# A hybrid decoder trunk on one core: S5 steps let in by VectorE's account, and initial states copied by ScalarE

## The chip, the cores and the metric

The kernel runs on one core of one Trainium2 chip. The metric is the device time of one execution in microseconds (us), as the median of the runs shown; lower is better. The profile is of one execution of its own. Engines: PE is TensorE (with its weight loads as PEld), DVE is VectorE, ACT is ScalarE, POOL is GpSimd, and SP is the engine that issues most DMAs.

## The reference, cut to what matters

Two layers (DEPTH 2) run over 256 prompt tokens and 8 sample streams of 4 tokens, 288 tokens in all, with a model width of 2048, in float32.

```python
def _layer(x, ...):
    z = x @ w_in
    u, cv, cg = z[..., :1024], z[..., 1024:2048], z[..., 2048:]
    y5, h_re, h_im = _s5(u, h0_re, h0_im, ...)   # diagonal complex state space, 64 groups x 64 states
    g5 = gelu(y5); s5_out = g5 * sigmoid(g5 @ s5_w_glu)
    c = silu(_ln(_causal_dwconv(cv * sigmoid(cg), conv_buf, conv_w, conv_b)))   # width 31
    x = _ln(ALPHA * x + concatenate([s5_out, c]) @ w_out)
    gate, val = split(_causal_dwconv(x @ ffn_w_up, ffn_buf, ...))               # width 3
    x = _ln(ALPHA * x + (silu(gate) * val) @ ffn_w_down)
    x = _ln(ALPHA * x + sigmoid(x @ pe_w_gate) * (p @ pe_w))
```

The S5 part is h[t] = a h[t-1] + B u[t], y = Re(C h) + D u, with complex a. The prompt starts at h = 0; each sample stream starts at its own state h0.

## The kernel before

**Weights.** All weights stream through SBUF in units of eight 128x128 blocks (512 KB), `wraw`, with four buffers. ScalarE rounds a unit to `whi` (L202) and VectorE makes the rest `wlo` (L145, the line of a helper that records every VectorE instruction). A block costs three matmuls on 288 columns (L379, L384, L385). The first ten units of layer 0 go without a split, in plain float32 matmuls (L375).

**Order.** One Python program writes the order of every engine's queue by hand. It keeps three accounts in nanoseconds. `pe_t` is TensorE's: 400 for a block, 485 for a plain one, 1000 for `inject`, 1500 for `project`, 400 for `s5_steps`, 500 for each of the 8 steps of a convolution. `dve_t` adds up VectorE's instructions and is what S5 steps pay with. `dve_c` says when VectorE would be done with all that it was given:

```python
cost = 150.0 + (2.1 if name == "tensor_tensor_scan" else 1.05) * n
self.core.dve_c = max(self.core.dve_c, self.core.pe_t) + cost
```

So `dve_c - pe_t` is the length of VectorE's list by the account. Until now it only decides when the load of the next `wraw` is written into SP's queue (`freed`).

**S5.** Beside the weight blocks runs a generator, `s5`. Every second block, `tick` (L259 and after) first runs timers (`at`), then lets the generator make steps while its budget `scan[2]` is above zero; the budget grows with `pe_t` at `rate` (3 during the set-up in layer 0, then 1.05 and 0.9 in the two layers). A step that has nothing to do yields None and ends the loop until the next tick. The S5 width is cut in 8 chunks `c`. A chunk goes through: the tables `em`, `om`, `kp` from raw weights (layer 0 only; in layer 1 they were made ahead during the FFN of layer 0 and are loaded); `load_u`; `inject` (PE, `bu`); `scan` (DVE: two products with a rotation `stb`, a scan, two products, then the shifted states `hin`); `project` (PE, `y`); `gelu`; a trip through DRAM (`y_d`) back into `u32`. `scan` waits until `project` of the chunk before is in the queue, `inject` of the next chunk follows `scan`, and `project(c)` waits until the table of the chunk has come back (`state["o"]`): two timers of 7000 and 8000 after the copies `om` (L973), which themselves wait for `project(c-1)`.

The initial states of the 8 sample streams are put into the last 8 columns of `hin`: two GpSimd copies of 128x32 per chunk (L1029), then VectorE writes the other columns.

**Around it.** The same stretch holds the Conformer part: per chunk two products, a GLU on VectorE into `cbuf` (L145), its trip through DRAM (POOL: `cb_d`, `stack`), and a convolution on TensorE (L1215, L1218). After the last S5 chunk come the half-GLU matmuls (`g`), which need each chunk's gelu output split into `xh`, `xl`; `finish(scan)` and `xs_g` run the generator without asking for its budget if it is late. Layer 0's S5 stretch lies at about 58 to 240 us, layer 1's at about 1423 to 1584 us.

Of the kernel before, what the change touches and what calls it, by code (L numbers as in the profile page):

```python
# [10 lines left out]
AF = mybir.ActivationFunctionType  # L11
# [39 lines left out]
RATE = (1.05, 0.9)  # L51
SETUP_RATE = 3
BANK = 1400.0
TICK = 2
U_LAG = 8000.0
BACK_LAG = 7000.0
# [102 lines left out]
class Core:  # L159
# [60 lines left out]
    def next_block(self):  # L220
        s, o = divmod(self.pos, SB)
        if o == 0:
# [4 lines left out]
            self.sub.pop(s - 1, None)  # L227
        if o % TICK == 0:
            if s < NATIVE:
# [29 lines left out]
    def tick(self):  # L259
        for x in self.late:  # L260
            x[0] -= 1
        while self.late and self.late[0][0] <= 0:
            self.late.pop(0)[1]()
        while self.freed and self.freed[0][1] <= self.pe_t:
            self.stream_dma(self.freed.pop(0)[0])
        self.run_timed()
        if self.scan:
            self.scan[2] = min(self.scan[2] + self.rate * (self.pe_t - self.pe_l), BANK)
            while self.scan and self.scan[2] > 0 and self.step(self.scan):
                pass  # L270
        self.pe_l = self.pe_t
        for b in list(self.bg):
            if b is self.scan:
                continue
            b[2] = min(b[2] + b[1], 2 * b[1])
            while b[2] > 0 and self.step(b):
                pass
# [582 lines left out]
    def s5(self, l, mp):  # L860

        nc, a = self.nc, self.a
        V, G = self.V, nc.gpsimd
        N4 = 4 * NCH

        def once(n, shp):
            return mp.tile(shp, F32, name=n, tag=n, bufs=1)
        fin = once("fin", [P, NPAIR, 2, 9])
        h0 = once("h0", [P, NPAIR, 2, NB])
# [6 lines left out]
        H = once("hin", [P, 2, 4, NCH])  # L876
# [9 lines left out]
        def work(shp):  # L886
            while finals:
                finals.pop(0)()
            n = 1
            for d in shp[1:]:  # L890
                n *= d
            t = mp.tile([P, 2 * N4], F32, tag="sw", name="sw", bufs=4)[:, :n]
            if len(shp) == 3:
                return t.rearrange("p (a b) -> p a b", b=shp[2])
            return t.rearrange("p (a b c) -> p a b c", b=shp[2], c=shp[3])
# [111 lines left out]
        def scan(c, v, tb):  # L1007
            shp = [P, 2, N4]
            cosb, sinb = [tb[:, k:k + 1].to_broadcast(shp) for k in range(2)]
            A, B = work(shp), work(shp)  # L1010
            V.tensor_tensor(A, v[:, :, :N4], cosb, OP.mult)
            V.tensor_tensor(B, v[:, :, :N4], sinb, OP.mult)
            yield 1.0
            V.tensor_tensor(A[:, 0], A[:, 0], B[:, 1], OP.add)
            V.tensor_tensor(A[:, 1], A[:, 1], B[:, 0], OP.subtract)
            yield 1.0
            Af = A.rearrange("p r t -> p (r t)")
            V.tensor_tensor_scan(Af, d0.rearrange("p r q n -> p (r q n)"), Af, 0.0, OP.mult, OP.add)
            yield 1.0
            V.tensor_tensor(B, A, cosb, OP.mult)  # L1020
            yield 1.0
            V.tensor_tensor(A, A, sinb, OP.mult)
            yield 1.0
            Av, Bv = [t.rearrange("p r (q n) -> p r q n", n=NCH) for t in (A, B)]
            e = SEQ // STEP
            while state["p"] < c - 1:
                yield None
            for i in range(2):
                G.tensor_copy(H[:, i, :, e:], h0[:, 4 * c:4 * c + 4, i])  # L1029
            V.tensor_tensor(H[:, 0, :, 1:e], Bv[:, 0, :, 0:e - 1], Av[:, 1, :, 0:e - 1], OP.subtract)  # L1030
            V.tensor_tensor(H[:, 1, :, 1:e], Av[:, 0, :, 0:e - 1], Bv[:, 1, :, 0:e - 1], OP.add)
            yield 1.0

            def final():
                f = fin[:, 4 * c:4 * c + 4]
                G.tensor_tensor(f[:, :, 0, 0:1], Bv[:, 0, :, e - 1:e], Av[:, 1, :, e - 1:e], OP.subtract)
                G.tensor_tensor(f[:, :, 1, 0:1], Av[:, 0, :, e - 1:e], Bv[:, 1, :, e - 1:e], OP.add)
                for i in range(2):
                    G.tensor_tensor(f[:, :, i, 1:], f[:, :, i, 1:], Bv[:, i, :, e:], OP.add)
            finals.append(final)  # L1040
# [63 lines left out]
        def main():  # L1104
            if l == 0:
                yield from self.wait(M0_LAG)
            G.memset(om, 0.0)
            tb = tables(0)
            initial()
            for c in range(S5C):  # L1110
                while c not in ready or state["e"] < c:
                    yield None
                self.rate = RATE[l]
                v = inject(us[c])
                state["i"] = c
                yield from self.wait(PS_LAG)
                yield from scan(c, v, tb)
                if c + 1 < S5C:
                    tb = tables(c + 1)
                streams.insert(0, tail(c, us.pop(c)))  # L1120
# [511 lines left out]
```

## Time and profile before

| what | value |
|---|---|
| median of 3 runs | 2739.69 us (2739.51 to 2741.52) |
| profiled execution, its own time | 2743.43 us |
| span in its profile | 2741.6 us |
| mean granted TensorE clock | 0.991 |
| busy share: PE, DVE, ACT, POOL | 97%, 66%, 49%, 11% |

The span runs from the first to the last instruction. A granted clock of 1.00 is 2.4 GHz, and 0.50 is 1.2 GHz; a window's value between them is a mean. Idle time of an engine is put down to the instruction or DMA that ended the wait ("<-"); "issue" means that nothing which the profile shows ended it.

### The profile page before, as it was taken

The numbers are of one execution on the slowest core, as the hardware profiler recorded it, in microseconds if no ns is written. First come the engines' busy times: TensorE is split into PE (matmuls) and PEld (weight loads), VectorE is DVE, ScalarE is ACT, GpSimd is POOL, SyncE is SP. The second block draws the span as 40 slices with busy tenths as digits, with TensorE's granted clock in tenths as the row PEclk, the third lists the DMA queues.
The fourth block names the chain that finished last, engine by engine and source line by source line (L and its number), as shares of the span: only waits on it lengthen the run. The fifth ranks groups of instructions, "written<-read, shape, count | busy, mean of one in ns | idle before, by whom it ended". The sixth has DMA issues, their size and how long they took to land. (4 is left out here: it accounts for less than half of the span.)

```text
span 2741.6 us, 57943 instructions
## 1 busy us (share of the span) xinstructions
PE 2660.2 (97%) x23696; PEld 2600.8 (95%) x23696; DVE 1808.4 (66%) x3016; ACT 1352.9 (49%) x2224; POOL 305.0 (11%) x913
## 2 busy tenths in 40 slices
PE   8898999999999999999998899999999999999997
PEld 7887999999999999999987889999999999999997
DVE  6885768665677546667876558676546664566686
ACT  3453547553455345546464435565435553455363
POOL 3442001000011000000034410010000000000000
PEclk9999999999999999999999999999999999999998
DMA  7988444456566654554468775445554555455442
GB/s 236 254 249 248 151 153 162 162 192 190 186 190 197 201 167 159 174 172 153 164 191 257 229 204 180 154 159 171 175 169 157 169 174 171 156 169 176 164 151 102
DMA packets 188042, 496.12 MB, mean 181 GB/s; under 512 B 46369, under 2 KB 72241, under 8 KB 187521
## 3 DMA queue, kind: packets, MB, share of 16 engines
q1 hardware_dynamic: 174592, 444.00, 49.9%
q0 software_dynamic: 13184, 48.42, 6.2%
q8 instruction: 186, 3.05, 0.5%
q14 instruction: 80, 0.65, 0.1%
HBM read 472.11 MB, written 24.87 MB: 181 GB/s over the span
## 5 line engine op out<-in xcount | busy, mean ns | idle before, releaser
L379 PE MATMUL acc<-xh,whi 128*128 128x288 f32 x4656 | 1377.4, 296 | 8.1 <-ACT e L1333 3.2
L384 PE MATMUL acc<-xl,whi 128*128 128x288 f32 x4357 | 1288.0, 296 | 4.6 <-issue 3.7
L385 PE MATMUL acc<-xh,wlo 128*128 128x288 f32 x4357 | 1286.4, 295 | 0.0
L202 ACT ACTIVATE whi<-wraw 128x1024 fp32r<-128x1024 f32 x766 | 791.8, 1051 | 344.7 <-PE acc L384 206.1
L145 DVE TENSOR_TENSOR wlo<-wraw,whi 128x1024 fp32r<-128x1024 f32 x766 | 921.3, 1225 | 41.6 <-ACT whi L202 23.9
L379 PEld LDWEIGHTS acc<-xh,whi 128*128 128x128 f32 x4656 | 877.7, 189 | 15.8 <-ACT e L1333 4.1
L385 PEld LDWEIGHTS acc<-xh,wlo 128*128 128x128 f32 x4357 | 820.5, 188 | 3.9 <-issue 3.9
L384 PEld LDWEIGHTS acc<-xl,whi 128*128 128x128 f32 x4357 | 820.7, 188 | 3.0 <-DVE xl L145 2.5
L379 PE MATMUL acc<-hh,whi 128*128 128x288 f32 x1408 | 416.3, 296 | 0.0
L145 DVE SCALAR_TENSOR_TENSOR fo<-fe,parf,fo 128x304 f32<-128x304 f32 x352 | 188.2, 535 | 323.0 <-ACT fo L1366 316.6
L385 PE MATMUL acc<-hh,wlo 128*128 128x288 f32 x1312 | 387.7, 296 | 0.0
L384 PE MATMUL acc<-hl,whi 128*128 128x288 f32 x1312 | 386.9, 295 | 0.0
L379 PEld LDWEIGHTS acc<-hh,whi 128*128 128x128 f32 x1408 | 265.2, 188 | 0.5
L384 PEld LDWEIGHTS acc<-hl,whi 128*128 128x128 f32 x1312 | 247.0, 188 | 0.0
L385 PEld LDWEIGHTS acc<-hh,wlo 128*128 128x128 f32 x1312 | 246.6, 188 | 0.0
L1362 ACT ACTIVATE fe<-acc 128x256 f32<-128x256 f32 x176 | 67.4, 383 | 290.2 <-PE acc L385 290.2
L1372 POOL COPY fstage<-fe 128x9 f32<-128x9 f32 x176 | 44.5, 253 | 1038.1 <-ACT fe L1363 1016.7
L438 ACT ACTIVATE ln_q<-x 128x288 f32<-128x288 f32 x90 | 40.1, 446 | 221.1 <-DVE x L145 221.1
L1366 ACT ACTIVATE fo<-fe,parf 128x304 f32<-128x304 f32 x176 | 113.1, 642 | 16.7 <-ACT fe L1363 0.4
L145 DVE TENSOR_TENSOR x<-x,acc 128x288 f32<-128x288 f32 x64 | 29.1, 454 | 139.1 <-PE acc L385 139.0
L1386 ACT ACTIVATE hh<-fth 128x288 fp32r<-128x288 f32 x88 | 39.2, 445 | 163.5 <-DVE fth L145 163.5
L145 DVE SCALAR_TENSOR_TENSOR x<-x,acc 128x288 f32<-128x288 f32 x64 | 29.0, 453 | 122.9 <-PE acc L385 122.8
(251 smaller groups left out, 2340.7 us busy)
## 6 DMA issues: line engine op xcount, KB each, us to landing
wraw<-in_wts_dram SPq DMA_DIRECT2D x776, 512.0 KB
stack<-cb_d POOLq DMA_DIRECT2D x32, 282.0 KB, 9.3
cw<-in_convw_dram POOLq DMA_DIRECT2D x16, 512.0 KB, 5.3
big<-cb_d POOLq DMA_DIRECT2D x24, 282.0 KB, 9.6
cbuf<-in_convi_dram POOLq DMA_DIRECT2D x16, 283.5 KB, 9.6
cb_d<-cbuf POOLq DMA_DIRECT2D x16, 283.5 KB, 3.6
out_dram<-cb_d POOLq DMA_DIRECT2D x16, 283.5 KB, 11.5
sbt<-in_s5b_dram SPq DMA_DIRECT2D x15, 256.0 KB
```

The source lines that it names most:

```text
L145: return f(out, *args, **kw)
L202: self.nc.scalar.activation(hi, self.raw[s], AF.Copy)
L379: nc.tensor.matmul(out, w[0], xh, start=first, stop=False)
L384: nc.tensor.matmul(out, w[0], xl, start=False, stop=False)
L385: nc.tensor.matmul(out, w[1], xh, start=False, stop=last)
L438: nc.scalar.activation(st["q"], v, AF.Square)
L1362: nc.scalar.activation(e[:, 2:2 + SEQ], acc[:, :SEQ], AF.Copy)
L1366: nc.scalar.activation(o[:, :w], e[:, 2:EW], AF.Identity, bias=self.prm("ffn_conv_b", m), scale=self.prm("ffn_conv_w2", m))
L1372: nc.gpsimd.tensor_copy(stage[:, z, :, 0], e[:, SEQ:EW:6])
L1386: nc.scalar.activation(hh[i], h, AF.Copy, scale=0.5)
```

## The change

The loop in `tick` gets one more condition: a step of S5 is made only while VectorE's list by the account is under 7000 ns. The two copies of initial states go from GpSimd to ScalarE. Nothing else changes; the steps of `finish` and `xs_g` and of the generator that makes layer 1's tables ahead don't ask for the new condition.

```diff
+BACKLOG = 7000.0
 ...
-            while self.scan and self.scan[2] > 0 and self.step(self.scan):
+            while self.scan and self.scan[2] > 0 and self.dve_c - self.pe_t < BACKLOG and self.step(self.scan):
                 pass
 ...
             for i in range(2):
-                G.tensor_copy(H[:, i, :, e:], h0[:, 4 * c:4 * c + 4, i])
+                nc.scalar.activation(H[:, i, :, e:], h0[:, 4 * c:4 * c + 4, i], AF.Copy)
```

## Rows read from the trace of the kernel before

**Rows 1.** What TensorE waited for, 58 to 240 us: total, times, longest.

```profile
PE bu L399 <- ACT em L947: 4.9, 4, 4.0
PE bu L399 <- DMA ust<-u_d: 4.2, 3, 2.9
...
PE bu L399 <- DMA tm<-k_d: 2.0, 1, 2.0
PE y L399 <- ACT kp L812: 1.6, 1, 1.6
```

**Rows 2.** Windows: length, busy us of PE, PEld, DVE, ACT, POOL, clock, DMA share, GB/s.

```profile
58.00:83.00 25.00, 22.35 (x361) 21.23 (x361) 21.17 (x38) 8.57 (x14) 10.35 (x19) 0.93 1.00 276
83.00:108.00 25.00, 20.87 (x289) 19.65 (x288) 21.80 (x37) 11.27 (x21) 9.87 (x22) 0.86 0.94 259
...
128.00:153.00 25.00, 20.55 (x389) 17.34 (x388) 17.66 (x35) 10.81 (x21) 10.04 (x19) 0.93 0.82 247
...
58.00:240.00 182.00, 164.10 (x2843) 148.53 (x2843) 145.97 (x255) 82.97 (x156) 80.58 (x150) 0.96 0.90 253
```

**Rows 3.** What SP's queue waited for, 58 to 240 us.

```profile
SPq L186 <- DVE wlo L145: 36.1, 12, 6.3
```

**Rows 4.** VectorE's groups, shapes apart, 62 to 218.2 us: count | busy, mean ns | idle before.

```profile
L145 DVE TENSOR_TENSOR wlo<-wraw,whi 128x1024 fp32r<-128x1024 f32 x28 | 35.4, 1264 | 1.7 <-ACT whi L202 1.6
...
L145 DVE TENSOR_TENSOR sw<-scc,aP 128x512 f32<-128x512 f32 x14 | 9.1, 686 | 4.8 <-DMA scc<-in_s5c_dram 4.2 <-POOL fin L1037 0.6
...
L145 DVE TENSOR_TENSOR ln_s<-cvo,cvo 128x288 f32<-128x288 f32 x1 | 0.5, 458 | 0.0
```

**Rows 5.** TensorE's groups in the same stretch.

```profile
L379 PE MATMUL acc<-xh,whi 128*128 128x288 f32 x224 | 70.0, 312 | 2.2 <-issue 2.2
...
L399 PE MATMUL bu<-ust,em 128*32 128x72 f32 x448 | 10.5, 242 | 10.6 <-ACT em L947 4.9 <-DMA ust<-u_d 3.6 <-DMA tm<-k_d 2.0
```

**Rows 6.** Groups of VectorE and of TensorE in layer 1, 1427 to 1582 us.

```profile
L145 DVE TENSOR_TENSOR wlo<-wraw,whi 128x1024 fp32r<-128x1024 f32 x30 | 38.0, 1275 | 10.1 <-ACT whi L202 8.2 <-PE bu L399 2.0
...
L145 DVE TENSOR_TENSOR hin<-sw 128x252 f32<-128x252 f32 x16 | 9.5, 633 | 0.6 <-PE y L399 0.5
...
L379 PE MATMUL acc<-xh,whi 128*128 128x288 f32 x239 | 72.5, 303 | 0.0
```

**Rows 7.** VectorE's groups, 8 to 33 us (set-up).

```profile
L145 DVE SCALAR_TENSOR_TENSOR stack<-stack 128x64 f32<-128x64 f32 x21 | 4.7, 222 | 0.7
```

**Rows 8.** TensorE's waits, 20 to 60 us.

```profile
PE tp L710 <- DVE em L145: 0.6, 1, 0.6
```

**Rows 9.** Tiles kps and y (0 to 300 us): ns min/median/max, first and last start.

```profile
L807 PE MATMUL kps<-pw,bsm x256: 217/219/317, 50.2 to 946.3; 128*32 128x64 f32 x128
...
L399 PE MATMUL y<-ust,tm x256: 226/226/251, 80.5 to 233.5; 128*32 128x72 f32 x128
```

**Rows 10.** ScalarE's groups, 58 to 240 us.

```profile
L786 ACT ACTIVATE pw<-scc 128x64 f32<-128x64 f32 x7 | 1.7, 241 | 0.0
```

**Rows 11.** Tile hin, 1420 to 1590 us; columns as in rows 9, last line a wait.

```profile
L1029 POOL COPY hin<-h x16: 199/575/1270, 1430.1 to 1576.4; 128x32 f32<-128x32 f32 x16
L145 DVE TENSOR_TENSOR hin<-sw x16: 409/438/1054, 1431.4 to 1579.4; 128x252 f32<-128x252 f32 x16
...
PE y L399: 2.9, 1
```

**Rows 12.** Timelines of VectorE, then TensorE, at the half-GLU: start, us, instruction.

```profile
259.72 0.46 DVE L145 TENSOR_TENSOR xl<-u,xh 128x288 fp32r<-128x288 f32 x1
...
267.74 0.29 PE L379 MATMUL acc<-xh,whi 128*128 128x288 f32 x1
```

**Rows 13.** Timelines of SP and of ScalarE: start, us, instruction.

```profile
120.73 11.04 SPq L1071 DMA_DIRECT2D u<-y_d  x4
...
92.61 0.68 ACT L996 ACTIVATE stb<-stb 128x576 f32<-128x576 int32 x1 [3.67 <-POOL stb L990]
```

**Rows 14.** ScalarE in layer 1: start, us, instruction.

```profile
1453.69 0.69 ACT L996 ACTIVATE stb<-stb 128x576 f32<-128x576 int32 x1 [7.51 <-POOL stb L990]
```

## The prediction

> **What bounds the kernel now.** I read the page first: TensorE is busy 97% of the span, so only its idle time and its time at the low clock can be won. Of the waits listed for TensorE over the whole span, most of what is not the start, the layer norms or the end stands in the two S5 stretches, so I read those by themselves.
>
> In layer 0, from 58 to 240 us, TensorE waits for things that S5 prepares: em, the loaded ust, the table behind tm, kp: 4.9 + 4.2 + 2.0 + 1.6 = 12.7 us [rows 1]. Each longer wait also costs clock. The windows show a granted clock of 0.93, 0.86 and 0.93 in three stretches of 25 us that hold the three waits of 2.0, 4.0 and 2.9 us, so in each a part ran at 1.2 GHz instead of 2.4: 25 x (0.07 + 0.14 + 0.07) = 7.0 us [rows 2]. Together 19.7 us, 0.7% of the time, is what the gate could win there.
>
> Is VectorE's lag behind these waits? It is busy 146 of the 182 us [rows 2]. SP's queue waits 36.1 us in it for wlo, because a load of wraw stands in the queue until VectorE has freed its buffer [rows 3]. One more hold, at 120.73, is for y_d, which VectorE's gelu must write first: it keeps SP for 11.04 us, and the ust that TensorE misses at 138.8 is queued behind it [rows 13]. So a late VectorE makes loads late, on a queue where nothing can pass.
>
> **The gate: when it closes.** I add up the account by its own formula, an instruction 150 + 1.05 ns an element (2.1 for the scan). It is near the truth: 1225 for wlo against 1264 measured, 217 against 222 for a 64-element one [rows 4, 7]. Over the 23 groups of 62 to 218.2 us, of which first, one and last stand, the work is 136.3 thousand ns: 28 wlo are 34.3, S5 94.5, the rest 7.5 [rows 4]. TensorE's account moves on in the same stretch by 224 blocks x 400 + 7 inject x 1000 + 7 project x 1500 + 7 table steps x 400 + 4 convolutions x 4000 = 125.9 thousand [rows 5] (project, tables and convolutions are counted alike in the groups not shown). So the list grows by 10.4 thousand, from about 2 thousand at the start: it is over 7000 for good in the second half, and before that in the bursts, since the tables of a chunk (5.9 thousand) and its scan (6.1) fall due close together. The gate closes here, in every chunk from about the third on.
>
> In layer 1, where no tables are made, the same sum gives 97.6 thousand of work against 129.5 [rows 6] (with the groups not shown): the list stays under 7000 in the S5 stretch and the gate stays open. It is shut for some time at that layer's start, where the layer norm's splits make a list, but S5 only waits for its first u there.
>
> In the set-up of layer 0 (from 8 us) eleven steps of together 19.9 thousand ns come one per tick of 970 ns, beside 452 ns of splits every second tick [rows 7]. Adding tick by tick, the list passes 7000 at the seventh step, and some 7 ticks are held: the set-up ends about 6.8 us later.
>
> **What a later step costs.** The set-up's delay is covered: the first table step runs at 50.2 us and the first project at 80.5 [rows 9], and 15 us of timers lie between, so 15 us of room against 6.8. If that cover were gone it would cost the 6.8. It also spaces out the small instructions before tp, which now waits 0.6 us for one of them [rows 8]: 0.6 won.
>
> In the main stretch a held step moves all that it issues: per chunk on SP the four loads of ust, six of the raw tables, four of tm, four of u; on POOL k_d and y_d; on TensorE bu, kps and y. They go behind weight loads, GLU trips and convolutions that so far stood behind them. The list may not exceed 7000 plus a step, where it ends near 12 now: S5 finishes some 5 us later. Its last y starts at about 232 [rows 9], the split of that chunk is written at 260.2 and first needed at 267.7 [rows 12], so 7.6 us are free, and more, as timers that the forced steps skip lie between. Cost 0.
>
> **What the gate wins.** Three waits I put down to VectorE's list: bu at 70.8 (2.0, VectorE stood for the raw tables scc, 4.2 us in all [rows 4], before it read the last bu) with 1.75 of clock; ust at 138.8 (2.85) with 1.75; kp (1.55). Together 9.9 us. The longest, em at 94.3 (4.0, with 3.5 of clock), I don't count: ScalarE stood 3.67 us for POOL's stb before it [rows 13], and POOL for the GLU's trip. Bounds: 0 and 19.7. Against that, moving so many steps makes waits of its own. Nothing shows them; the bounds are 0 and again 20, and I take one of the middle size seen, 2.0 + 1.75, rounded to 3.7.
>
> **The copies.** 32 copies leave POOL, and 32 reach ScalarE at 0.24 us (64 elements took 241 ns [rows 10], and 32 are taken at the same; the bounds are 0 and that): 7.7 us on an engine that is busy 83 of 182 us [rows 2]. They are queued behind the om copies, which wait for the same project, so they add no wait of their own; behind them stand gelu and the next whi. If that cover is gone, 7.7 is the price. What they win: TensorE waited once, 2.9 us, for such a copy [rows 11]. But right behind it bu needs em, and ScalarE was held there till 1453.69 by stb from the same POOL queue [rows 14]. The wait moves on to bu; only the copies' own length ahead of stb goes, 0.35 us.
>
> The row of tile hin shows POOL's copy at 199 to 1270 ns and VectorE's write at 409 to 1054 for one shape each, so the two engines delay one another [rows 11]. The Trainium skill ("SBUF — State Buffer", section "Who interferes with whom") says that VectorE with two SBUF inputs and a GpSimd instruction that reads SBUF exclude each other for a whole instruction; the spread agrees. By that rule alone VectorE gets back 16 x (633 - 409) ns = 3.6 us in layer 1 [rows 6, 11], and if all of it lay on TensorE's path the copies would be worth 3.6 instead of 0.35.
>
> **The sum.** -9.9 - 0.6 - 0.35 + 3.7 = -7.15 us. On the profiled execution, 2743.43, that makes 2736.3; the median stands 3.74 lower, so 2739.69 - 7.15 = 2732.5.
>
> **The rivals.**
>
> A, same: the list is shorter only on paper. The account leaves out TensorE's stalls, so real VectorE was busy 80% only, and the DMAs were busy 0.82 to 1.00 of three windows [rows 2]: loads may be late whatever VectorE does. Then S5 is reshuffled, old waits go and as many come: 2739.7 less the small terms, about 2738.
>
> B, slower: the chain of a chunk runs out of room. A chunk takes (233 - 81) / 7 = 21.8 us now, of which 15 are timers; project and om poll once a tick, and a closed gate keeps each poll waiting. If that adds 4 us a chunk, S5 ends 28 us later; with 7.6 us free and some 12 that forced steps get back from timers it decides from 20 us on, and TensorE waits the remaining 8 in the half-GLU: 2748. Against it: between bursts the list drains faster than one tick per tick.
>
> C, slower: the ScalarE copies lie on the path: +7.7, 2747. For it: ScalarE feeds whi and every eviction. Against it: it is idle half of the stretch.
>
> D, much faster: all of layer 0's S5 waits and clock go, with no new one: -19.7 - 0.95, 2719.
>
> E, same: the gate does nothing of note and the port alone counts: -3.6 - 0.6, 2735.5.
>
> **Numbers.** Forecast 50% (its own range 2726 to 2734), A 20%, E 5%, B 10%, C 8%, D 7%. A measurement tells 0.2%, 5.5 us, from no change: faster is under 2734.2, slower over 2745.2. Faster 0.50 + 0.07 = 0.57; same 0.25; slower 0.18. The range leaves out half of D and a part of B and C: 2720 to 2746.
>
> **What would show it.** Right: in 58 to 240 us TensorE's waits for em, ust, tm and kp fall from 12.7 to under 8, the clock of the windows rises, SP's waits for wlo fall well under 36; the first table step is near 57 instead of 50 us and the first project stays near 80; the last y comes 3 to 10 us later with no wait in the half-GLU; the waits of layer 1's stretch stay, with bu in hin's place. Wrong: new waits over 2 us for ust or stb in layer 0 (A), a wait over 4 us for u or its split near 265 us (B), whi or em late with ScalarE busy before it (C).

## The result, and the profile after

The changed kernel takes 2766.24 us, median of four executions from 2765.02 to 2770.24; the kernel before, run beside it, 2739.60. The ratio is 1.0097, 95% interval 1.0084 to 1.0110: 26.6 us slower. The forecast was 2732.5, the range 2720 to 2746; the result lies above the range and above both rivals on the slow side (2747 and 2748). The profiled execution's span is 2763.2 us against 2741.6, at a mean granted clock of 0.985 against 0.991.

TensorE's waits from 58 to 272 us (layer 0's S5 stretch ends later here), then over layer 1's stretch, 1420 to 1580 us (total, times, longest):

```profile
PE y L400 <- DMA tm<-k_d: 14.8, 4, 5.7
PE kps L808 <- DVE bsm L146: 7.5, 1, 7.5
PE bu L400 <- ACT em L948: 6.6, 6, 4.4
...
PE bu L400 <- ACT em L948: 11.5, 4, 11.1
PE bu L400 <- DMA wraw<-in_wts_dram: 4.7, 1, 4.7
PE bu L400 <- DMA ust<-u_d: 2.2, 1, 2.2
```

Against [rows 1]: the waits for ust (4.2) and kp (1.6) are gone, as forecast. In their place stand two kinds that were hardly there: the first table step kps waits 7.5 us for its input, and the projection y waits four times, 14.8 us in all (the last of them, 4.7 us, behind 240 us), for the loaded table tm, where one wait of bu, 2.0, stood. In layer 1 one wait of 11.1 us for em is new.

The same windows as in [rows 2], and one of layer 1, which starts 13.2 us later here (its first store of u is issued at 1421.3 us instead of 1408.1); the last line is the kernel before, 13 us earlier:

```profile
58.00:83.00 25.00, 21.16 (x272) 20.03 (x273) 21.99 (x43) 13.18 (x26) 6.06 (x10) 0.80 0.69 199
83.00:108.00 25.00, 20.46 (x273) 19.49 (x272) 18.76 (x30) 10.04 (x21) 14.76 (x26) 0.89 0.99 241
128.00:153.00 25.00, 19.27 (x309) 17.66 (x312) 14.39 (x28) 10.28 (x21) 4.97 (x9) 0.86 0.81 224
58.00:240.00 182.00, 159.06 (x2635) 146.47 (x2639) 145.49 (x259) 84.65 (x173) 71.72 (x121) 0.93 0.84 236
...
1440.00:1513.00 73.00, 54.88 (x875) 50.48 (x874) 39.95 (x57) 28.80 (x56) 28.45 (x52) 0.86 0.74 209
```

```profile
1427.00:1500.00 73.00, 64.83 (x1112) 60.15 (x1112) 49.15 (x68) 34.21 (x58) 37.19 (x71) 0.98 0.87 263
```

TensorE gets through 2635 matmuls in the 182 us where it did 2843, at a clock of 0.93 instead of 0.96. Around each new wait part of a window runs at 1.2 instead of 2.4 GHz: the mean clock is 0.80 in the 25 us that hold the end of the wait for kps (TensorE idle for 7.5 us up to 61.8), and 0.86 in layer 1's window, with 875 matmuls, where the kernel before has 0.98 and 1112.

SP's queue in the stretch of [rows 3], and the tiles kps and y of [rows 9]:

```profile
SPq L187 <- DVE wlo L146: 27.5, 11, 4.6
SPq L1072 <- DMA y_d<-yw: 21.4, 3, 12.0
SPq L923 <- DMA k_d<-kp: 20.9, 2, 11.6
...
L808 PE MATMUL kps<-pw,bsm x128: 218/219/316, 61.8 to 242.2; 128*32 128x64 f32 x128
...
L400 PE MATMUL y<-ust,tm x256: 223/226/330, 85.9 to 265.9; 128*32 128x72 f32 x128
```

The hold for wlo is shorter (27.5 against 36.1); holds for y_d (10.6 in the kernel before) and k_d (0.6) have taken its place. S5 starts 11.6 us later (kps 61.8 against 50.2) and ends 32 us later (last y 265.9 against 233.5).

### The profile page after: what moved, and what is told of

Its sections match the earlier page's. It is cut to its first block, busy times and chain, and to the rows that moved or that the text cites. A ratio compares the mean times of both kernels' runs of the same rounds, so it can differ in the third digit from the quotient of the medians.

```text
span 2763.2 us, 57930 instructions
## 1 busy us (share of the span) xinstructions
PE 2667.5 (97%) x23696; PEld 2609.4 (94%) x23696; DVE 1806.9 (65%) x3016; ACT 1356.5 (49%) x2256; POOL 292.0 (11%) x881
## 4 chain that ended last, share of the span: by engine, by line
PE 86%; DMA 6%; DVE 3%; issue 2%; ACT 1%; POOL 1%; SPq 0%; ACTq 0%; DVEq 0%; POOLq 0%
PE acc L380 27%; PE acc L385 25%; PE acc L386 25%; PE acc L362 2%; PE acc L382 2%; DMA wraw<-in_wts_dram 2%; PE acc L1216 1%; PE acc L376 1%; DMA cbuf<-in_convi_dram 1%; DMA ust<-u_d 1%; DVE wlo L146 1%; DVE sw L146 1%; DMA sqb<-q_d 1%; DMA y_d<-yw 1%; DMA sbt<-se_d 1%
```

## The experiments

All are timed side by side with the kernel before; the ratio goes by those runs. One execution differs from the next by several us, so differences under 3 us between experiments say nothing. A profile is of one execution too, and that one can lie several us from its kernel's median. Three theories stood at the start: S, the gate holds back the start-ups of the layers, and what they load comes late; M, steps held in the running chunks come late against timers that run on; C, the copies on ScalarE lie on the path.

**Which edit, and which phase.** Four kernels part the change. `going` is false from a layer's start to its first inject.

```diff
copies_only   - ... and self.dve_c - self.pe_t < BACKLOG and ...
gate_only     + G.tensor_copy(H[:, i, :, e:], h0[...])     (copies on GpSimd again)
gate_running  + ... (not self.going or self.dve_c - self.pe_t < BACKLOG) ...
gate_starts   + ... (self.going or self.dve_c - self.pe_t < BACKLOG) ...
```

> The gate is left out, the copies stay on ScalarE. Theory C (the ScalarE copies lie on the path): about 2747, up to 7.7 us above before, so a third of the loss. Theory S (the start-ups held by the gate) and theory M (steps held in the running chunks come late against fixed timers): 2735 to 2740, no loss at all, the wait of TensorE for the copied tile replaced by one for em in layer 1.

> The gate stays, the copies go back to GpSimd. Theory C: 2758 or less. Theories S and M: 2764 to 2768, as the changed kernel, and a wait over 9 us for em at the start of layer 1's stretch again.

> The gate counts only from a layer's first inject on, so the set-up and both start-ups run as before. Theory S: the loads of sqb land near 41 us again, kps loses its wait of 7.5 us and bu in layer 1 its 11.1 us; with their clock (half of 10.2 less 3.8, and half of 13.7 less what before had there) that is some 9 us in layer 0 and 7.5 us in layer 1: 2750 or less, and if S is all of it 2737 to 2742. Theory M: 2760 to 2766, the last y still near 263 us and four waits of y for tm.

> The gate counts only until a layer's first inject; the running chunks are as before. Theory S: 2756 to 2766, with kps waiting about 7.5 us and em in layer 1 about 11 us. Theory M: 2738 to 2744, the late start being made up by timers that stand between the steps. If both hold a part, this run and the one with the gate in the running chunks alone share the loss of 26.6 us.

Measured: copies_only 2738.44 us, ratio 0.9998 (0.9986 to 1.0011); gate_only 1.0093 (1.0073 to 1.0112); gate_running 1.0029 (1.0018 to 1.0041), 8 us; gate_starts 1.0068 (1.0050 to 1.0086), 18.6 us. The copies cost and win nothing that could be measured; theory C falls. The loss is the gate's, and both its phases have a part: 0.29 + 0.68 is the whole 0.97%. Both times fall where theory S put them, so the starts carry the larger part; but M's mechanism is there too. TensorE's waits of gate_running, 58 to 272 us:

```profile
PE y L401 <- DMA tm<-k_d: 9.3, 3, 3.4
PE bu L401 <- ACT em L949: 8.0, 4, 5.3
```

The waits of y for tm stay, 9.3 us in three. The order of the instructions of SP, VectorE, ScalarE and GpSimd in its trace differs from that of copies_only in layer 0 alone, so in layer 1's running chunks the gate did not close.

The trace of copies_only, which has no gate, bears on what the gate was to win. TensorE's waits, 58 to 240 us:

```profile
PE bu L400 <- ACT em L948: 8.4, 5, 5.0
...
PE y L400 <- ACT kp L813: 1.4, 1, 1.4
PE bu L400 <- DMA ust<-u_d: 0.7, 1, 0.7
```

The queues of SP and VectorE have the order of the kernel before. Still ust stands at 0.7 instead of 4.2, tm at nothing instead of 2.0, and em at 8.4 instead of 4.9. So waits of this size come and go without the gate, and the going of one in a gated kernel is not by itself the gate's work.

**Which start.** The same gate up to the first inject, in one layer each; then each with its first or its last part exempt. `<list is short>` stands for the gate's own condition.

```diff
gate_setup_l0     + (self.lay or self.going or <list is short>)
gate_start_l1     + (not self.lay or self.going or <list is short>)
gate_setup_steps  as gate_setup_l0, with `self.going = True` right behind `yield from self.setup(mp)`
gate_l1_after_u   + (not self.lay or self.going or not self.u_d or <list is short>)
```

> The gate counts in layer 0 until its first inject and nowhere else. The run with the gate in both start-ups lost 18.6 us. If both layers' starts share it as the trace of that run has it (kps 6.7 us late and its half clock, against em 9.0 us late in layer 1 and its half clock): 2745 to 2750. If the layer-0 start is made up by the timers behind it: 2737 to 2741. If it carries all of the start-ups' loss: 2755 or more.

> The gate counts in layer 1 until its first inject and nowhere else. By the trace of the run with both start-ups, in which layer 1 grew by some 11 us over before: 2746 to 2751, with bu waiting some 9 to 11 us for em of the second chunk. If layer 1's loss there came only with the changes of layer 0: 2737 to 2741.

> As the run with the gate in layer 0's start, but the gate ends with the last step of the set-up on VectorE; the loads of sqb, the table steps and the first copies of em that follow are let in at once. If the late set-up itself is the cost: the time of that run, within 2 us, kps again 6 to 7.5 us late. If the hold on the steps behind the set-up is the cost: 2737 to 2742, kps late by under 2 us.

> As the run with the gate in layer 1's start, but steps are let in freely until the layer's first u is written, so the generator's own first step (loads of h0 and sqb, memsets, the first table on GpSimd) runs at the layer's start as before. If the late first step on GpSimd is what makes the second em late: 2737 to 2741, no wait over 4 us for em. If it is the hold on the copies and loads that follow the first u: the time of that run, within 2 us.

Measured: gate_setup_l0 1.0023 (1.0011 to 1.0035), 6 us; gate_start_l1 1.0020 (1.0008 to 1.0031), 5.5 us; gate_setup_steps 1.0033 (1.0020 to 1.0046); gate_l1_after_u 1.0023 (1.0011 to 1.0034). Both starts cost. In layer 0 it is the held set-up itself, not what is held behind it; in layer 1 it is the hold on what follows the first u, not the late first step on GpSimd. Alone the two make 0.43%, together 0.68 +/- 0.18; the intervals do not tell whether the rest is real.

**Layer 0: what the late set-up costs.** Two remedies on gate_setup_steps: the loads of sqb put ahead of the stores of u_d on GpSimd's queue, or the first table step put later in TensorE's.

```diff
gate_setup_q_first   -            if l == 0:
                     -                yield from self.wait(Q_LAG)
gate_setup_kps_late  -                yield from self.wait(PJ_LAG)
                     +                yield from self.wait(PJ_LAG + (9000.0 if c == 0 else 0.0))
```

> The gate holds only the set-up's VectorE steps in layer 0, as in the run before (8 us lost), but the four loads of sqb are put on GpSimd's queue ahead of the four stores of u_d. Theory queue order (the late set-up costs because sqb's loads fall behind stores that wait for the first u, and behind the convolution's loads): sqb lands near 46 us instead of 52 to 57, kps loses most of its 7.9 us wait, and 2738 to 2743. Rival, the late set-up costs by itself (less time than the timers promised): 2746 or more, kps still 5 us late or later.

> The set-up's steps are held as in the run that lost 8 us, but the first chunk's table step (kps) is put 9000 ns of TensorE's account later in TensorE's queue, about where its data came in that run. If the loss is TensorE standing in its in-order queue for a table that a timer has put there too early: the wait of 7.9 us goes and 2738 to 2743. If the loss is the chunk chain of layer 0 being later as a whole: the wait goes and the time stays at 2745 or more, with new waits further on.

Measured: q_first 1.0022 (1.0011 to 1.0033); kps_late 0.9998 (0.9990 to 1.0007). GpSimd's queue in the changed kernel, then in q_first (start, us, instruction, idle before it):

```profile
36.20 1.22 POOL L718 DMA_DIRECT2D q_d<-em  x2 [30.22 <-DVE em L146]
41.75 2.17 POOL L1173 DMA_DIRECT2D u_d<-u  x4 [4.33 <-ACT u L1171]
43.91 0.54 POOL L1226 DMA_DIRECT2D cbuf<-in_convi_dram  x1
44.44 2.42 POOL L752 DMA_DIRECT2D sqb<-q_d  x4
```

```profile
36.71 1.23 POOL L719 DMA_DIRECT2D q_d<-em  x2 [30.73 <-DVE em L146]
42.18 2.41 POOL L753 DMA_DIRECT2D sqb<-q_d  x4 [4.25 <-DMA q_d<-em]
44.54 2.26 POOL L1175 DMA_DIRECT2D u_d<-u  x4
```

In the kernel before, q_d went out at 32.74, sqb at 36.42 and u_d only at 43.80. The store of q_d is 3.5 us later in the changed kernel, and sqb, now emitted after u_d, stands behind stores that wait for the first u: 8.0 us later. A load of sqb then takes 7.2 us to land (median of four) against 2.2 before, while the DMAs are busier (share 0.90 from 44 to 56 us, against 0.63 from 35 to 41 us in the kernel before). The loads of the kernel before, then of the changed one (KB each, us to landing):

```profile
sqb<-q_d POOLq DMA_DIRECT2D x4, 64.0 KB, 2.2
```

```profile
sqb<-q_d POOLq DMA_DIRECT2D x4, 64.0 KB, 7.2
```

The Trainium skill ("DMA: Bandwidth & Descriptors", section "Anatomy of one DMA — SWDGE (gpsimd) path") gives about 2.0 us plus the bytes over 436 thousand per us for such a load, an estimate of 2.15 us for 64 KB; the row of before agrees, the one after does not.

In q_first a load lands in 3.5 us, yet kps still waits 8.3 us, and the time, 2744.71 us, lies between the two ranges; it falls by less than the intervals resolve (1.0022 against 1.0033). VectorE's first step on sqb and its last for kps in q_first:

```profile
48.45 1.02 DVE L146 TENSOR_TENSOR sw<-sqb,sbt 128x512 f32<-128x512 f32 x1 [5.21 <-DMA sqb<-q_d]
...
58.44 0.73 DVE L146 TENSOR_TENSOR bsm<-sw 64x64 f32<-64x64 f32 x4
```

Two things used up what the earlier loads gave. From 48.45 to bsm's end VectorE takes 10.7 us, where the changed kernel takes 6.6 for the same instructions; GpSimd is busy beside it from 47.3 to 58.0, while in the changed kernel GpSimd is done at 54.4, before these steps begin. And the timer that q_first leaves out also put kps later in TensorE's queue: TensorE reaches kps at 50.9 us, against 55.5 in gate_setup_steps. So this run does not test the queue's order by itself.

Putting kps later mends the loss: it runs at 73.5 us without a wait, and nothing is lost, though TensorE now stands 4.8 us for wlo, which is queued on VectorE behind the table's steps. Its last y comes at 244.8 us, 11 later than before, at no cost (these rows are of the slowest of its eleven executions, 2746.30 us).

VectorE shows where the room was that the prediction counted on. The kernel before, last operand of kps; then the changed one:

```profile
47.01 1.38 DVE L145 TENSOR_TENSOR bsm<-sw 64x64 f32<-64x64 f32 x4
```

```profile
44.66 1.23 DVE L146 TENSOR_TENSOR wlo<-wraw,whi 128x1024 fp32r<-128x1024 f32 x1 [2.25 <-ACT whi L203]
55.25 0.69 DVE L146 TENSOR_TENSOR sw<-sqb,sbt 128x512 f32<-128x512 f32 x1 [9.36 <-DMA sqb<-q_d]
...
61.10 0.72 DVE L146 TENSOR_TENSOR bsm<-sw 64x64 f32<-64x64 f32 x4
```

Before, bsm is done at 48.39 and kps runs at 50.2 [rows 9]: 1.8 us of room. After, VectorE stands 9.36 us for sqb, bsm ends at 61.82, 13.4 us later, and kps starts then. The place of kps has moved too, by 4.1 us (TensorE reaches it at 54.3), so 13.4 - 1.8 - 4.1 = 7.5 us, the wait.

**Layer 1: what the late start costs.** The gate counts only from the issue of the first load of sbt on:

```diff
gate_l1_after_load  + (not self.lay or self.going or not self.ready or <list is short>)
                    + self.ready = True      (behind ge = load_e(0, nc.gpsimd, bt0))
```

> The gate counts in layer 1 only between the issue of the first load of sbt and the first inject. The two runs that gated this start lost 5 to 6 us, with sbt put on GpSimd's queue behind all four stores of u_d. Theory queue order: with sbt ahead of them again the loss goes, 2736 to 2741, em of the second chunk waits under 4 us for sbt. Rival, the held copies and table loads that follow cost: 2743 to 2748.

Measured: 0.9995 (0.9986 to 1.0004). The loss goes. Queues of gate_start_l1: first GpSimd, then SP and GpSimd for the second chunk, and ScalarE's em that waits:

```profile
1406.53 2.14 POOL L1176 DMA_DIRECT2D u_d<-u  x4 [240.36 <-ACT u L1174]
...
1411.88 0.54 POOL L915 DMA_DIRECT2D sbt<-se_d  x1
...
1425.18 2.22 POOL L1192 DMA_DIRECT2D stack<-cb_d  x4 [3.08 <-DMA cb_d<-cbuf]
...
1427.77 0.39 SPq L915 DMA_DIRECT2D sbt<-se_d  x1
...
1438.96 1.33 ACT L949 ACTIVATE em<-sbt,mask 128x512 f32<-128x512 f32 x2 [9.62 <-DMA sbt<-se_d]
```

The same of gate_l1_after_load:

```profile
1405.29 0.59 POOL L1177 DMA_DIRECT2D u_d<-u  x1 [18.04 <-ACT u L1175]
1405.88 0.54 POOL L915 DMA_DIRECT2D sbt<-se_d  x1
1406.40 1.61 POOL L1177 DMA_DIRECT2D u_d<-u  x3
...
1421.07 0.41 SPq L915 DMA_DIRECT2D sbt<-se_d  x1
1423.61 2.21 POOL L1193 DMA_DIRECT2D stack<-cb_d  x4 [3.33 <-DMA cb_d<-cbuf]
...
1427.87 1.33 ACT L949 ACTIVATE em<-sbt,mask 128x512 f32<-128x512 f32 x2 [2.82 <-DMA sbt<-se_d]
```

The first load of sbt, ahead of three of u_d's four stores or behind all four, sets the whole chain of the second one. Where it is early, the second load is issued 2.5 us ahead of the four loads of the convolution's stack, and em starts 6.8 us after the issue. Where it is late, it is issued 2.6 us behind them, and em starts 11.2 us after it, having held ScalarE for 9.6. On SP's queue the load has the same neighbours in both, loads of wraw; what differs is GpSimd's. In the changed kernel it is issued 1.6 us behind the stack and em starts 12.7 us after, which is TensorE's wait of 11.1:

```profile
1440.91 2.21 POOL L1189 DMA_DIRECT2D stack<-cb_d  x4 [3.54 <-DMA cb_d<-cbuf]
...
1442.46 0.38 SPq L914 DMA_DIRECT2D sbt<-se_d  x1
...
1455.18 1.33 ACT L948 ACTIVATE em<-sbt,mask 128x512 f32<-128x512 f32 x2 [11.04 <-DMA sbt<-se_d]
```

The Trainium skill ("PSUM — Partial Sum Buffer", section "Engine vs sequencer instructions") calls the queues of ScalarE, VectorE and GpSimd strictly first in, first out; the rows of GpSimd and ScalarE here agree.

**The running chunks: which of the held things costs.** Each kernel has holds of its own in the generators instead of the gate; all act after a layer's first inject.

```diff
+ def held(self, g):                       # list long: yield None; else next(g)
gate_tables       + yield from self.held(self.s5_into(m, bt, qb))
                  + yield from self.held(self.s5_out(l, c, cc, bc, pw, bs, work))
gate_scans        + yield from self.held(scan(c, v, tb))
gate_both         both of these
gate_loads_tails  + streams = [self.held(loads()), prep(), main()]
                  + streams.insert(0, self.held(tail(c, us.pop(c))))
gate_scans_4000   gate_scans with BACKLOG = 4000.0
scans_held_pool_copies   gate_scans with the copies on GpSimd
```

> The gate is a hold of its own in layer 0's table steps on VectorE (into and out) after the first inject; start-ups, loads, scans, projections and tails run freely. Theory timers (the gate in the running chunks costs because the tables come late, k_d late after them, and tm later than the projection): 2744 to 2750, y waiting for tm of k_d by 5 us or more in sum. Rival, what costs is that loads and projections themselves are held: 2737 to 2741.

> The same hold in the scan's steps alone. Theory timers: 2737 to 2742, since the scan's result is awaited by the projection, which is waited for by a timer of 6000 ns, and k_d is not late. Rival, any late VectorE step costs: 2744 to 2750. If the forecast of the prediction were right somewhere, it would be here: 2730 to 2735.

> Layer 0's table steps and scan steps are both held by the list after the first inject, each by its own hold, while loads, projections and tails run freely. If the 8 us of the gate in the running chunks come from VectorE's steps being late together (a held table is waited for by a scan that is then held too): 2744 to 2750. If they come from the loads, projections and tails that the gate holds as well: 2731 to 2739, at or under the run with the scans alone.

> The opposite: after the first inject only the loads of u and the tails (projection, gelu) are held by the list, while no step of tables and scans is. If holding loads and projections is what costs: 2743 to 2750. If VectorE's own late steps cost: 2736 to 2741.

> The hold of the scans alone with the bound at 4000 instead of 7000. If the shorter list is what gained 4 to 6 us there, it is held more often and gains as much or more: 2726 to 2734. If the scan's chain has no room for more, y comes late: 2738 to 2746. If the gain at 7000 was one lucky order of instructions: anything near 2739.

> The hold of the scans alone at 7000, with the copies back on GpSimd. If the gain of that run is the hold's: again 2731 to 2736, 0.1 to 0.35% under before. If it was the ScalarE copies in that order of instructions, or chance: 2737 to 2742.

Measured: gate_tables 0.9995 (0.9981 to 1.0009); gate_scans 0.9978 (0.9965 to 0.9990); gate_both 1.0042 (1.0029 to 1.0056); gate_loads_tails 0.9985 (0.9973 to 0.9997); gate_scans_4000 1.0015 (1.0006 to 1.0023); scans_held_pool_copies 0.9987 (0.9977 to 0.9998). It is neither the tables alone (the timers' theory missed there) nor the loads and projections (2733.29 us, under both of its ranges), but both of VectorE's parts held together. In gate_tables SP stands 7.8 us for k_d (0.6 in the kernel before) and the last y comes at 246.0, but TensorE waits for tm no longer than before (2.0); why y waits only when the scans are held as well, no run shows. Waits of TensorE, 58 to 272 us, in gate_both, then in gate_scans:

```profile
PE bu L411 <- ACT em L959: 13.6, 7, 7.3
PE y L411 <- DMA tm<-k_d: 7.9, 3, 4.0
```

```profile
PE bu L411 <- ACT em L959: 7.7, 6, 5.8
...
PE y L411 <- DMA tm<-k_d: 0.7, 1, 0.7
```

Window 58 to 240 us and the last y of gate_scans, then the last y of gate_both:

```profile
58.00:240.00 182.00, 169.89 (x2916) 155.57 (x2910) 146.58 (x257) 88.63 (x178) 72.67 (x135) 0.98 0.92 266
...
L411 PE MATMUL y<-ust,tm x256: 223/226/251, 78.2 to 233.7; 128*32 128x72 f32 x128
```

```profile
L411 PE MATMUL y<-ust,tm x256: 223/226/328, 78.5 to 253.2; 128*32 128x72 f32 x128
```

With the scans alone held the chain ends where it did before (233.7 against 233.5), TensorE gets through 2916 matmuls instead of 2843 and the clock is 0.98 instead of 0.96 [rows 2]. These rows make the difference too large: the profiled execution of gate_scans, 2726.39 us, is the fastest of its twelve, that of the kernel before, 2743.43, lies above its median. With both held the chain ends 20 us later. With the bound at 4000 the last y slips to 246.5 as well and 4 us are lost; the longest new waits there are for wlo (8.6 us in two), not for y. The gain by the two runs at 7000 is 3.6 and 6 us. Both intervals lie under 1, the second only just, and its 2737.34 us falls into the range that was put down for chance. gate_loads_tails came out as far below 1 as that one, so part of such a gain, or all of it, may be no more than another order of the instructions.

**A version by another reading.** The longest waits left are bu's for em; ScalarE had stood for GpSimd's stb before them [rows 13, 14]. So, in the kernel before, its sine over stb was put later:

```diff
- self.at(2500.0, lambda: nc.scalar.activation(f, tb, AF.Sin, ...))
+ self.at(2500.0 if c == 0 else 7000.0, sine)      (and at the scan at the latest)
```

> No gate, copies on GpSimd, as before; ScalarE's sine over the tables is put 7000 ns of TensorE's account behind their making on GpSimd instead of 2500, from the second chunk on. If TensorE's longest waits in the S5 stretches (bu for em) come from ScalarE standing in its own queue for the GpSimd table, and that for a convolution's round trip: the waits of 4 to 5 us near 94 us and 3 to 8 us near 1455 us go, and with their clock 2728 to 2735. If em is late by its own chain: 2737 to 2741.

Measured: 0.9999 (0.9987 to 1.0011). Nothing is won. In its trace ScalarE no longer stands for stb ahead of the em at 92 us, but 1.1 us for VectorE's sw, and TensorE still waits 3.2 us for that em, where it was 4.0; so standing for stb is not what that wait came from. In layer 1 the wait for hin stays (3.1 us). The only versions whose intervals lie under 1 are those with held scans (0.9978 and 0.9987) or held loads and tails (0.9985).

## Why the prediction was wrong

**Right.** The gate closes in layer 0's chunks and stays open in layer 1's, as the sum of the account had it. The copies cost nothing (0.9998; 216 ns each against the 240 taken), and in layer 1 the wait moved on from hin to em. The 3.6 us of rival E's port did not come: without the copies on GpSimd VectorE's writes of hin in layer 1 take 650 ns in the mean (copies_only), 633 before. The scans held alone give -3.6 and -6 us where -7 was forecast, but that is another change than the one forecast, and no support for its sum.

**Not shown: "What the gate wins", 9.9 us.** The waits for ust and kp went and SP's hold for wlo shrank, but without the gate (copies_only) the waits for ust and tm were as good as gone too and the hold was 31.7. And one reading behind the 9.9, worth 4.6 of it, was wrong. The hold on SP at 120.73 was put down to a late y_d. GpSimd issues that store earlier, and its stores between 100 and 150 us land within 5.1 us, so y_d was there before the hold began:

```profile
114.45 0.56 POOL L1065 DMA_DIRECT2D y_d<-yw  x1 [0.95 <-DVE yw L145]
```

One of SP's four issues took 7.4 us there; why, the profile does not say.

**Wrong: "The set-up's delay is covered ... 15 us of room".** This is the first of three steps that failed. The 15 us were timers (7000 and 8000) that lie behind kps, between the copies of om and project. They can cover a late projection, not a late kps, whose place in TensorE's queue another timer fixes. The room of kps is the time from its data's being ready to that place: 1.8 us. The set-up's last store slipped by 3.5 us, not 6.8, yet bsm slipped by 13.4, since sqb was issued 8.0 us later and took 5 us longer to land. The text gave the price with the cover gone as 6.8; measured alone it is 6 to 9 us, and kps put later takes it away, so what costs is that kps stands in TensorE's queue ahead of its data. How much of the 13.4 is the queue's order and how much the busier DMAs stays open: in q_first, with the order mended, bsm was still 10.8 us late.

**Wrong: "S5 only waits for its first u there"** (layer 1's start, the second step). The generator also issues the first load of sbt there, between two stores of u_d. Held until after them, it drags the second load behind the convolution's stack: 5.5 us alone, nothing when the load is let through.

**Wrong: main stretch, "Cost 0"** (the third). S5 was to end 5 us later with 7.6 us free. The last y came 18 us later with the running gate alone (251.6) and 32 us in the whole change. Rival B had this mechanism, a chain whose polls are held, but put the wait in the half-GLU and its price at 8 us in sum. There is room at the end, 11 us at least (gate_setup_kps_late). The price shows earlier: y stands for tm, whose store k_d follows the held table while y's place is kept by timers; with the tables alone held, k_d was late too but y did not wait, so the held scans have a part that is not explained. That is 8 us. The one "wait of its own" in the sum, 3.7, stood for 14.8 us of waits for tm and their clock.

The sum was thus wrong on what a held step moves, and what it gave the gate as won no run bears out. Alone the three phases make 8 + 6 + 5.5 = 19.5 us of the 26.6. The other 7 lie between the two starts together (18.6) and apart (11.5), a difference that the intervals hardly tell from nothing; no run here says whether it is real.

## What to carry to other kernels

A timer between two emissions is no slack: read the slack from the trace, from the end of the last operand to the start of its first reader, before anything upstream is delayed. A step that is held keeps its loads back too, and on first-in-first-out queues they come out behind stores that wait for something else and behind bulk transfers; list each queue's neighbours before and after the move. A throttle on a generator that also issues loads holds the loads too; put it on the instructions that make the load it watches, and only where their readers have room. Here a hold on the scans alone was the only hold on VectorE's steps that may have won something, 3.6 to 6 us. And before a wait that has gone is put down to a change, see whether it stays in a kernel without the change.

## What was not expected of the hardware

The time from a load's issue to the instruction that waits for it differed with what was queued around it. The second sbt of layer 1 took 6.1 and 6.8 us when issued 2.6 and 2.5 us ahead of four stack loads of 282 KB (copies_only, gate_l1_after_load), and 9.4, 11.2 and 12.7 us when issued 4.3, 2.6 and 1.6 us behind them (gate_l1_after_u, gate_start_l1, the changed kernel). A load of sqb landed in 2.2, 3.5 or 7.2 us. And VectorE took 10.7 us beside a busy GpSimd for the steps from sqb to bsm that took it 6.6 without.
